# FFN of a two-layer hybrid decoder step: where the sums of the weight blocks stand in VectorE's and ScalarE's queues

## The chip, the cores and the metric

The kernel runs on one core of one Trainium2 chip (trn2). The metric is the time of one execution in device microseconds; of several runs the median is taken. A profiled execution is one further run, taken by the hardware profiler, and its time differs a little from the median.

## The reference

The program is one inference step of a small decoder: layer 0 mixes tokens with an mLSTM, layer 1 with latent attention, and behind each stands a SwiGLU FFN. There are 1024 prompt tokens and 8 new tokens of sampled sequences; in the kernel they stand side by side, 1032 columns. Only the FFN is touched by the change:

```python
def swiglu(x, w_gate_up, w_down):
    g, u = jnp.split(x @ w_gate_up, 2, axis=-1)
    return (jax.nn.silu(g) * u) @ w_down

hp = hp + swiglu(rmsnorm(hp, norm_ffn[layer]), ffn_w_gate_up[layer], ffn_w_down[layer])
hs = hs + swiglu(rmsnorm(hs, norm_ffn[layer]), ffn_w_gate_up[layer], ffn_w_down[layer])
```

Everything is float32. The model width is 1024, the FFN's inner width is 2816, that is 22 blocks of 128.

## The kernel before

**Arithmetic.** A float32 product is made of three matmuls in the format fp32r: both operands are split into a high part (ScalarE, `split`, L117: a copy that rounds) and a low part (VectorE, L118: source less high part), and `mm3` (L134 to L136) adds high x high, high x low and low x high. On top of that both projections of the FFN use a scheme of seven products for a 2 x 2 block product instead of eight (Strassen's, in Winograd's form): the seven left operands are four blocks of weights and sums of them, the seven right operands are blocks of activations and sums of them.

**Gate and up.** `gate_up(wg, f, parts, down)` makes block f of the 22 (called tile f here). Its two weight blocks, for gate and for up, are loaded by SyncE's queue into tiles `wr` (two buffers). From their quarters a11, a12, a21, a22 the function `operands` makes the seven operands: a11 and a12 as they are, then S = a21 + a22 (L1009) and S3 = a11 - a21 (L1010), S - a11 (L1014), a12 - S (L1017), and a22. Each is split into `wh`, `wl` or `w`. The order of the seven products is that of `PRODUCTS`: 0 and 4 (a11, a12), 3 (S - a11, here "the third product"), 1 (S), 2 (S3), 5 (a22), 6 (the last sum). Each product is made for two parts of the tokens, i = 0 (2 x 256 columns) and i = 1 (2 x 260), with 12 matmuls each, into PSUM banks `sc`. After each product the bank is read: by a copy on ScalarE (L1053, L1058, L1060) or by an instruction of VectorE (L1055, L1061, L1063, L1065, L1067); L1063 is the multiplication after product 5. The results are tiles `u`.

**Down.** The down projection takes the blocks of `u` in pairs (f, f + 1). `spread` makes the seven right operands `b` of a pair from its four `u` blocks by sums (L1075 to L1081) and splits. `down` is a generator: for each pair and each of four column blocks (a down tile) it makes 14 steps e, product e // 2 in the order of `PRODUCTS` for part e % 2, with 3 matmuls each, into banks `mm` and `ss`, and reads the banks (L1135 to L1146). The gate/up tile that runs at the time calls one step after every two of its groups of matmuls (28 steps a tile), so that the down projection of pair n runs in the middle of the gate/up tiles of later pairs; tile 3 calls them faster (54 steps). `down_raw` loads the weights of the next down tile into `dr` (one buffer) and makes their sums `dS` (L1096 to L1099) right behind it, at step 0; `down_put` splits A, B, D and C at steps 6, 9, 12 and 13. At the end of a down tile GpSimd issues a DMA that adds the result to the residual stream in memory (L1147).

**What sets the order.** Each engine works its queue strictly in order, and the order is made when the program is built: a scheduler takes the instructions by the order of the code and by its own estimate of when their operands are there. Where its estimate of a load is too short, an instruction stands in the queue ahead of others that could run. `tc.issue_after(ins)` orders every instruction made inside its block behind `ins` if it runs on the engine of `ins`; no wait on the chip comes with it.

**The start of the FFN.** `gate_up_half` makes tiles 0 and 1 for part 0 with plain products, and beside it VectorE and ScalarE make the right operands `c...` and `f...` of the other part from x (`forms`, L920 to L923; the last low half is `c5l`). Then `ffn` calls `spread` for the first pair's part 0, then tile 2 for both parts, then tiles 0 and 1 for part 1. Tiles `u` have four tags, and a tag is used again by a later block (`rows`).

Of the kernel before, what the change touches and what calls it, by code (L numbers as in the profile page):

```python
# [1 line left out]

# [1 line left out]

# [9 lines left out]
ALU = mybir.AluOpType  # L14
# [4 lines left out]
P = 128  # L19
D = 1024  # L20
KT = D // P
S = 1024
# [9 lines left out]
PW = (256, 260)  # L32
# [59 lines left out]
class Kern:  # L92
# [888 lines left out]


    def rows(self, f, i):
        x = self.t(self.gu, [P, 2, PW[1]], "u%d%d" % ((1, 0) if (f, i) == (0, 1) else (f % 2, i)))[:, :, :PW[i]]
        self.u[f, i] = x
        return x


    def operands(self, wg, f):
        nc = self.nc  # L990
        A = []
        for c0 in (f * P, DFF + f * P):
            raw = self.t(self.wp, [P, KT * P], "wr")
# [12 lines left out]

        G = nc.vector.tensor_tensor
        s, s3 = (self.t(self.gu, [P, 4, P], "S", bufs=2) for i in range(2))
        G(s, a21, a22, op=ALU.add)  # L1009
        G(s3, a11, a21, op=ALU.subtract)  # L1010
        yield put(a11)
        yield put(a12)
        s1 = put(s)
# [9 lines left out]
    def gate_up(self, wg, f, parts, down=iter(()), skip=0, steps=(1, 1)):  # L1023
# [8 lines left out]
        for s, bank, first in PRODUCTS:  # L1032
            ahead.append(next(ops, None))
            w = ahead.pop(0)
            for i in parts:
# [16 lines left out]
                if s == 0:  # L1052
                    nc.scalar.copy(u[:, 0], ps)  # L1053
                elif s == 4:
                    V.tensor_tensor(u[:, 0], u[:, 0], ps, op=ALU.add)  # L1055
                    nc.scalar.activation(u[:, 0], u[:, 0], AF.Silu)
                elif s == 3:
                    nc.scalar.copy(x, ps)  # L1058
                elif s == 2:
                    nc.scalar.copy(u[:, 1], ps)  # L1060
                    V.tensor_tensor(u[:, 1], u[:, 1], banks[i, 1], op=ALU.add)  # L1061
                elif s == 5:
                    V.tensor_tensor(u[:, 0], u[:, 0], ps, op=ALU.mult)  # L1063
# [23 lines left out]


    def down_raw(self, wd, f0, dp):
        nc = self.nc  # L1090
        G = nc.vector.tensor_tensor
        raw = self.t(self.fp, [P, 2, 2 * P], "dr")
        nc.sync.dma_start(raw, self.wsrc(wd, f0 * P, 2, dp * 2 * P, 2 * P))
        a11, a21, a12, a22 = (raw[:, k, r * P:r * P + P] for k in range(2) for r in range(2))
        S = self.t(self.fp, [P, 4, P], "dS")
        G(S[:, 1], a21, a22, op=ALU.add)  # L1096
# [3 lines left out]
        return {"A": raw[:, :, 0:P], "B": S[:, 0:2], "C": S[:, 2:4], "D": raw[:, 1:2, P:]}  # L1100


    def down_put(self, src, n):
# [6 lines left out]
    def down(self, wd):  # L1110
        nc = self.nc
        V = nc.vector
        todo = [(f0, dp) for f0 in range(0, NF - 4, 2) for dp in range(KT // 2)]
        src = self.down_raw(wd, *todo[0])
        W = {n: self.down_put(src, n) for n in "ABCD"}
        st0 = [self.t(self.wp, [P, KT * P], "wl", F32R).bitcast(F32) for _ in range(2)]
        yield
        for n, (f0, dp) in enumerate(todo):
# [7 lines left out]
            for e in range(14):  # L1126
# [11 lines left out]
                elif s == 3:  # L1138
                    nc.scalar.copy(c[:, 0, 1], ps)
                elif s == 2:  # L1140
                    nc.scalar.copy(c[:, 1, 1], ps)
                    V.tensor_tensor(c[:, 1, 1], c[:, 1, 1], banks[i][1], op=ALU.add)
                elif s == 5:
                    nc.scalar.copy(c[:, 1, 0], ps)
                elif s == 6:
# [873 lines left out]
```

## Time and profile before

| what | us |
|---|---|
| median of 3 runs | 2722.95 (2720.21 to 2729.66) |
| the profiled execution, whole | 2727.58 |
| its span, from the first to the last instruction | 2725.8 |
| TensorE (PE) busy | 2538.9 |
| VectorE (DVE) busy | 1859.1 |
| ScalarE (ACT) busy | 1327.4 |
| mean granted clock of TensorE | 0.973 of full |

In the profile's rows a line such as L1009 is a line of the kernel, `S<-wr` says which tile is written and which are read, buffer numbers left out. Times are counted from the start of the span. A matmul's busy time is modelled and overlaps the next one's start: in a full stretch a matmul with 256 columns is busy for 0.28 us and the next starts 0.12 us later. "[3.81 <-DMA wr]" is idle time of the engine ahead of this instruction, with what ended it. The first layer's FFN lies between about 536 and 1160 us, the second's between about 2012 and 2640 us.

### The profile page before, as it was taken

To read this page: it belongs to the slowest core of one execution; us is meant where nothing else is said; L and a number is where in the kernel's file an instruction comes from. 1 tells how busy PE (TensorE), PEld (TensorE's weight loads), DVE (VectorE), ACT (ScalarE), POOL (GpSimd) and SP (SyncE) were. 2 spreads that over 40 slices of the span, in tenths; PEclk is the share of its full clock that TensorE was granted. 3 is DMA by queue.
4 is the path that set the end of the run, shared out by engine and by line. 5 is a ranking of instruction groups with operands and counts; after the bars stand their busy time and mean duration, and the time that the engine had idled before them with its cause. 6 is when DMAs were issued, how large, how long until landed. Compare 5 with 4: busy or idle time off the path is not lost.

```text
span 2725.8 us, 54325 instructions
## 1 busy us (share of the span) xinstructions
PE 2538.9 (93%) x21151; PEld 2389.8 (88%) x21151; DVE 1859.1 (68%) x4490; ACT 1327.4 (49%) x3280; POOL 576.3 (21%) x582
## 2 busy tenths in 40 slices
PE   8999998989999999999887888888989999999998
PEld 8998887989999999999875667677789999999998
DVE  4345568887777777666556776768497777777755
ACT  4212234456555556453354455546255655655543
POOL 1000102201111111122334444442310111111102
PEclk9999989999999999999998999989999999999999
DMA  5133445526656656653666666653624755666553
GB/s 187 39 69 84 124 141 121 160 63 129 127 120 122 124 110 121 118 157 97 239 226 238 227 237 220 222 200 124 201 90 97 138 110 115 131 123 120 114 126 120
DMA packets 341992, 383.37 MB, mean 141 GB/s; under 512 B 23417, under 2 KB 274686, under 8 KB 333414
## 3 DMA queue, kind: packets, MB, share of 16 engines
q0 software_dynamic: 59520, 183.34, 28.8%
q1 hardware_dynamic: 257814, 180.21, 22.2%
q10 hardware_dynamic: 24400, 16.36, 2.4%
q8 instruction: 166, 2.72, 0.4%
q14 instruction: 92, 0.75, 0.1%
HBM read 254.12 MB, written 125.70 MB: 139 GB/s over the span
## 4 chain that ended last, share of the span: by engine, by line
PE 62%; DVE 16%; DMA 11%; ACT 5%; issue 3%; POOL 1%; another core or an unknown queue 0%; SPq 0%; ACTq 0%; POOLq 0%; DVEq 0%
PE sc L136 12%; PE sc L134 11%; PE sc L135 11%; PE mm L134 5%; PE mm L136 5%; PE mm L135 4%; DMA wr<-in_ffn_w_gate_up_dram 3%; DVE tt L1797 2%; PE ss L1829 2%; DMA Gb<-G_d 2%; PE ss L134 2%; PE ss L136 2%; PE ss L135 2%; DVE wl L118 2%; PE ss L1804 1%
## 5 line engine op out<-in xcount | busy, mean ns | idle before, releaser
L1147 POOL DMA_DIRECT2D x_d<-wl x72 | 86.7, 1205 | 1046.3 <-DVE wl L1146 367.4
L117 ACT ACTIVATE wh<-wr 128x512 fp32r<-128x512 f32 (+2 forms) x170 | 137.5, 810 | 225.5 <-PE mm L135 133.2
L1797 DVE STREAM_TRANSPOSE tt<-nat 128x1024 f32<-128x1024 f32 x128 | 153.9, 1223 | 9.5 <-PE ss L1804 6.1
L118 DVE TENSOR_TENSOR wl<-wr,wh 128x1024 fp32r<-128x1024 f32 (+2 forms) x83 | 99.8, 1203 | 39.5 <-ACT wh L117 31.2
L117 ACT ACTIVATE b<-u 128x256 fp32r<-128x256 f32 (+1 forms) x252 | 97.8, 414 | 43.6 <-DVE u L1063 29.7
L134 PE MATMUL mm<-zh,wh 128*128 128x344 f32 x320 | 105.3, 329 | 7.2 <-DVE ot L462 7.2
L1804 PE MATMUL ss<-tt,qbd 128*32 128x128 f32 x2560 | 92.7, 281 | 17.2 <-DVE tt L1797 12.2
L118 DVE TENSOR_TENSOR b<-u,b 128x256 fp32r<-128x256 f32 (+1 forms) x252 | 104.6, 422 | 1.4 <-ACT b L117 1.3
L135 PE MATMUL mm<-zl,wh 128*128 128x344 f32 x320 | 104.4, 326 | 0.0
L136 PE MATMUL mm<-zh,wl 128*128 128x344 f32 x320 | 104.2, 326 | 0.0
L1804 PEld LDWEIGHTS ss<-tt,qbd 128*32 128x32 f32 x2560 | 71.7, 112 | 34.0 <-DVE tt L1797 21.0
L1147 POOL DMA_DIRECT2D x_d<-st x72 | 99.1, 1376 | 4.4 <-DVE dC L118 3.5
L117 ACT ACTIVATE wh<-S 128x512 fp32r<-128x512 f32 x108 | 68.3, 633 | 47.7 <-PE sc L136 33.4
L118 DVE TENSOR_TENSOR wh<-S,wh 128x512 fp32r<-128x512 f32 x108 | 74.2, 689 | 22.1 <-ACT wh L117 21.0
L1700 PE MATMUL mm<-wh,vt 128*128 128x256 f32 (+1 forms) x320 | 75.6, 298 | 11.1 <-ACT wh L117 5.2
L134 PE MATMUL sc<-zh,wh 128*128 128x344 f32 x256 | 84.1, 329 | 1.3 <-ACT wh L117 1.1
L136 PE MATMUL sc<-zh,wl 128*128 128x344 f32 x256 | 83.3, 325 | 0.7 <-DVE wl L118 0.7
L135 PE MATMUL sc<-zl,wh 128*128 128x344 f32 x256 | 83.2, 325 | 0.0
L118 DVE TENSOR_TENSOR wh<-wr,wh 128x512 fp32r<-128x512 f32 x85 | 58.5, 688 | 26.5 <-ACT wh L117 26.4
L1659 ACT ACTIVATE wr<-sc,mx,rqt 128x512 f32<-128x512 f32 (+2 forms) x96 | 64.1, 673 | 22.5 <-DVE mx L1654 12.6
L1700 PEld LDWEIGHTS mm<-wh,vt 128*128 128x128 f32 x320 | 56.1, 197 | 21.6 <-ACT wh L117 8.7
L1789 POOL DMA_INDIRECT nat<-in_cache_latent_dram,idx x64 | 61.2, 957 | 61.8 <-PE ss L1829 48.2
(1052 smaller groups left out, 10703.2 us busy)
## 6 DMA issues: line engine op xcount, KB each, us to landing
wr<-in_ffn_w_gate_up_dram SPq DMA_DIRECT2D x96, 512.0 KB
x_d<-st POOLq DMA_DIRECT2D x72, 520.0 KB
x_d<-wl POOLq DMA_DIRECT2D x72, 512.0 KB
dr<-in_ffn_w_down_dram SPq DMA_DIRECT2D x72, 256.0 KB
wr<-in_mlstm_w_in_dram SPq DMA_DIRECT2D x24, 512.0 KB
wr<-in_mlstm_w_out_dram SPq DMA_DIRECT2D x16, 512.0 KB
wr<-in_mla_w_o_dram SPq DMA_DIRECT2D x15, 512.0 KB
q<-qn_d SPq DMA_DIRECT2D x28, 256.0 KB
```

The costliest lines, as they stand in the source:

```text
L117: ins = nc.scalar.activation(hi, src, AF.Copy)
L118: self.low = e.tensor_tensor(lo, src, hi.bitcast(F32), op=ALU.subtract)
L134: mm(ps, wh, xh, start=start, stop=False, **kw)
L135: mm(ps, wh, xl, start=False, stop=False, **kw)
L136: self.last = mm(ps, wl, xh, start=False, stop=stop, **kw)
L1147: nc.gpsimd.dma_start(self.x_d[:, 2 * dp:2 * dp + 2, 512 * i:512 * i + 2 * PW[i]], st[i], accum_op=ALU.add)
L1659: nc.scalar.activation(px[:, ks], o, AF.Exp, bias=mx[:, 0:1], scale=f, accum_out=sm[:, c:c + 1])
L1700: nc.tensor.matmul(o, x, y, start=i == 0, stop=i == len(ops) - 1)
L1789: nc.gpsimd.indirect_dma_start(out=nat[:, s].rearrange("p s c -> p (s c)"), out_offset=None, in_=lat, in_offset=ix)
L1797: V.transpose(out=tt, in_=src.rearrange("p s (c i) -> p c s i", i=32))
L1804: nc.tensor.matmul(psS[32 * j:32 * j + 32, u * P:u * P + P], self.qbd[:, b, cb], tt[:, c, 4 * j:4 * j + 4].rearrange("p s k -> p (s k)"), ...
L1829: nc.tensor.matmul(psV[32 * j:32 * j + 32], pz[:, j, i], keys[i // 4][:, j * 4 + i % 4], start=i == 0, stop=i == 7)
```

## The change

Four things are edited. In `operands` the first two sums S and S3 of every tile f > 3 are ordered behind `self.pin`, the multiplication after product 5 of part 0 of the tile before. In `down` the sums of the next down tile's weights are no longer made at step 0, with the load, but at step 8, ordered behind the two instructions (ScalarE's copy `y` and VectorE's addition `x`) that read the bank of that step; the split of A is made there too (it was at step 6), that of B at step 10 (it was at step 9). The first pair's combinations for part 0 are no longer called before tile 2: tile 2 gets them as its generator and calls one after every two groups of matmuls, from the seventh call on. And the tags of the tiles `u` are dealt out differently, so that tile 2 does not write to the buffers of the first pair.

```diff
     def rows(self, f, i):
-        x = self.t(self.gu, [P, 2, PW[1]], "u%d%d" % ((1, 0) if (f, i) == (0, 1) else (f % 2, i)))[:, :, :PW[i]]
+        x = self.t(self.gu, [P, 2, PW[1]], "u%d%d" % ((0, f) if f < 2 else (1 - f % 2, i)))[:, :, :PW[i]]
...
         s, s3 = (self.t(self.gu, [P, 4, P], "S", bufs=2) for i in range(2))
-        G(s, a21, a22, op=ALU.add)
-        G(s3, a11, a21, op=ALU.subtract)
+        with self.tc.issue_after(self.pin) if f > 3 else nullcontext():
+            G(s, a21, a22, op=ALU.add)
+            G(s3, a11, a21, op=ALU.subtract)
...
                 elif s == 5:
-                    V.tensor_tensor(u[:, 0], u[:, 0], ps, op=ALU.mult)
+                    ins = V.tensor_tensor(u[:, 0], u[:, 0], ps, op=ALU.mult)
+                    if i == parts[0]:
+                        self.pin = ins.ins
...
     def down_raw(self, wd, f0, dp):
         raw = self.t(self.fp, [P, 2, 2 * P], "dr")
+        self.nc.sync.dma_start(raw, self.wsrc(wd, f0 * P, 2, dp * 2 * P, 2 * P))
+        return {"A": raw[:, :, 0:P], "D": raw[:, 1:2, P:], "raw": raw}
+
+
+    def down_sums(self, src):
+        G = self.nc.vector.tensor_tensor
+        a11, a21, a12, a22 = (src["raw"][:, k, r * P:r * P + P] for k in range(2) for r in range(2))
         S = self.t(self.fp, [P, 4, P], "dS")
         G(S[:, 1], a21, a22, op=ALU.add)
         G(S[:, 0], S[:, 1], a11, op=ALU.subtract)
         G(S[:, 2], a11, a21, op=ALU.subtract)
         G(S[:, 3], a12, S[:, 0], op=ALU.subtract)
+        src.update(B=S[:, 0:2], C=S[:, 2:4])
...
                 elif s == 2:
-                    nc.scalar.copy(c[:, 1, 1], ps)
-                    V.tensor_tensor(c[:, 1, 1], c[:, 1, 1], banks[i][1], op=ALU.add)
+                    y = nc.scalar.copy(c[:, 1, 1], ps)
+                    x = V.tensor_tensor(c[:, 1, 1], c[:, 1, 1], banks[i][1], op=ALU.add)
...
                 if more and e == 0:
                     src = self.down_raw(wd, *todo[n + 1])
-                if more and e in (6, 9, 12, 13):
-                    x = {6: "A", 9: "B", 12: "D", 13: "C"}[e]
+                if more and e == 8:
+                    with self.tc.issue_after(x.ins), self.tc.issue_after(y.ins):
+                        self.down_sums(src)
+                        W["A"] = self.down_put(src, "A")
+                if more and e in (10, 12, 13):
+                    x = {10: "B", 12: "D", 13: "C"}[e]
                     W[x] = self.down_put(src, x)
...
-        for _, x, i in SPREAD:
-            if i == 0:
-                self.spread(0, x, i)
-        self.gate_up(wg, 2, (0, 1))
+        self.gate_up(wg, 2, (0, 1), (self.spread(0, x, i) for _, x, i in SPREAD if i == 0), 6)
```

GpSimd's and SyncE's instructions stand in the same order as before. On VectorE and ScalarE the FFN's instructions are reordered, on TensorE a few are.

VectorE's queue, before, around the sum S of gate/up tile 10 of the first layer (S_9224). Here u_8846 and u_8882 are tile 9's results for part 0 and part 1, wl_6158 and st_9049 the down projection's results, dA and dB its weights.

```order
L1061 TENSOR_TENSOR u_8882<-u_8882,sc_8915 128x260
L1009 TENSOR_TENSOR S_9224<-wr_9222 128x512
L118 TENSOR_TENSOR dA_9138<-dr_9056,dA_9138 128x256
L1010 TENSOR_TENSOR S_9225<-wr_9220,wr_9222 128x512
L1063 TENSOR_TENSOR u_8846<-u_8846,sc_8817 128x256
L118 TENSOR_TENSOR wh_9228<-wr_9220,wh_9228 128x512
L118 TENSOR_TENSOR b_9141<-u_8846,b_9141 128x256
L118 TENSOR_TENSOR b_9153<-u_8440,b_9153 128x256
L1063 TENSOR_TENSOR u_8882<-u_8882,sc_8849 128x260
L118 TENSOR_TENSOR wh_9231<-wr_9220,wh_9231 128x512
```

The same place of VectorE's queue in the changed kernel; line numbers from L1009 on are larger by one to seven there, u_8877 is what was u_8882, and L1064 is what was L1063.

```order
L1062 TENSOR_TENSOR u_8877<-u_8877,sc_8910 128x260
L118 TENSOR_TENSOR wh_9228<-wr_9220,wh_9228 128x512
L1064 TENSOR_TENSOR u_8846<-u_8846,sc_8817 128x256
L1010 TENSOR_TENSOR S_9224<-wr_9222 128x512
L1011 TENSOR_TENSOR S_9225<-wr_9220,wr_9222 128x512
L118 TENSOR_TENSOR b_9133<-u_8846,b_9133 128x256
L118 TENSOR_TENSOR b_9145<-u_8440,b_9145 128x256
L1064 TENSOR_TENSOR u_8877<-u_8877,sc_8849 128x260
L118 TENSOR_TENSOR wh_9231<-wr_9220,wh_9231 128x512
L118 TENSOR_TENSOR b_9168<-u_8477,b_9168 128x260
L118 TENSOR_TENSOR b_9182<-u_8877,b_9182 128x260
L1149 TENSOR_TENSOR wl_6158<-wl_6158,ss_9048 128x256
```

The low half of the first weights (wh_9228) and part 0's multiplication now stand ahead of the sum, the low half of dA (dA_9138 before) has gone behind it, and part 1's multiplication is still behind it.

TensorE's queue, before, at the first products of tile 2 of the first layer; sc_5649 and the other sc tiles are its banks, dA_6145 the down projection's first weights, b_5603 and b_5607 the first pair's right operands.

```order
L134 MATMUL sc_5681<-f4h_5074,w_5639 128x256
L135 MATMUL sc_5681<-f4l_5075,w_5639 128x256
L134 MATMUL sc_5696<-c4h_5574,w_5639 128x260
L135 MATMUL sc_5696<-c4l_5575,w_5639 128x260
L134 MATMUL mm_6225<-b_5603,dA_6145 128x256
L135 MATMUL mm_6225<-b_5603,dA_6145 128x256
L134 MATMUL ss_6226<-b_5607,dA_6145 128x256
L135 MATMUL ss_6226<-b_5607,dA_6145 128x256
L136 MATMUL sc_5649<-f0h_4927,wl_5636 128x256
L134 MATMUL sc_5649<-f0h_4927,wl_5636 128x256
```

The same place in the changed kernel (sc_5656 is what was sc_5681, sc_5671 what was sc_5696, wl_5611 what was wl_5636):

```order
L134 MATMUL sc_5656<-f4h_5074,w_5614 128x256
L135 MATMUL sc_5656<-f4l_5075,w_5614 128x256
L134 MATMUL sc_5671<-c4h_5574,w_5614 128x260
L135 MATMUL sc_5671<-c4l_5575,w_5614 128x260
L136 MATMUL sc_5624<-f0h_4927,wl_5611 128x256
L134 MATMUL sc_5624<-f0h_4927,wl_5611 128x256
```

The four matmuls with dA have gone to a later place, among the first products of tile 3; tile 2's own products follow each other.

VectorE's queue at the same time, before: c5l is the last low half of `forms`, wl_5636 the one that the matmul L136 above reads.

```order
L118 TENSOR_TENSOR c5l_5586<-x_4738,c5h_5585 128x1040
L1009 TENSOR_TENSOR S_5632<-wr_5630 128x512
L118 TENSOR_TENSOR b_5603<-u_5286,b_5603 128x256
L118 TENSOR_TENSOR b_5607<-u_5438,b_5607 128x256
L1075 TENSOR_TENSOR u_5286<-u_5286 128x256
L118 TENSOR_TENSOR b_5625<-u_5438,b_5625 128x256
L1079 TENSOR_TENSOR u_5286<-u_5438,u_5286 128x256
L118 TENSOR_TENSOR b_5610<-u_5286,b_5610 128x256
L1010 TENSOR_TENSOR S_5633<-wr_5628,wr_5630 128x512
L1077 TENSOR_TENSOR u_5286<-u_5438,u_5286 128x256
L118 TENSOR_TENSOR b_5619<-u_5286,b_5619 128x256
L1081 TENSOR_TENSOR u_5438<-u_5438,u_5286 128x256
```

And in the changed kernel:

```order
L118 TENSOR_TENSOR c5l_5586<-x_4738,c5h_5585 128x1040
L1010 TENSOR_TENSOR S_5607<-wr_5605 128x512
L1011 TENSOR_TENSOR S_5608<-wr_5603,wr_5605 128x512
L118 TENSOR_TENSOR wl_5611<-wr_5603,wl_5611 128x512
L118 TENSOR_TENSOR w_5614<-wr_5603,w_5614 128x512
L118 TENSOR_TENSOR wh_5617<-S_5607,wh_5617 128x512
L118 TENSOR_TENSOR b_5678<-u_5286,b_5678 128x256
```

Before, wl_5636 came next behind the last row shown, with nine instructions of the first pair and the two sums between c5l and it; now the two sums alone stand between, and the pair's instructions are behind.

More of the change, by code (lines that the diff above doesn't have):

```diff
@@ L1 @@
-from contextlib import ExitStack
+from contextlib import ExitStack, nullcontext
 import numpy as np
@@ L1089, in down_raw @@
     def down_raw(self, wd, f0, dp):
-        nc = self.nc
-        G = nc.vector.tensor_tensor
         raw = self.t(self.fp, [P, 2, 2 * P], "dr")
-        nc.sync.dma_start(raw, self.wsrc(wd, f0 * P, 2, dp * 2 * P, 2 * P))
-        a11, a21, a12, a22 = (raw[:, k, r * P:r * P + P] for k in range(2) for r in range(2))
+        self.nc.sync.dma_start(raw, self.wsrc(wd, f0 * P, 2, dp * 2 * P, 2 * P))
[3 more added lines that the diff above has]
+        a11, a21, a12, a22 = (src["raw"][:, k, r * P:r * P + P] for k in range(2) for r in range(2))
         S = self.t(self.fp, [P, 4, P], "dS")
@@ L1099, in down_raw @@
         G(S[:, 3], a12, S[:, 0], op=ALU.subtract)
-        return {"A": raw[:, :, 0:P], "B": S[:, 0:2], "C": S[:, 2:4], "D": raw[:, 1:2, P:]}
+        src.update(B=S[:, 0:2], C=S[:, 2:4])
     def down_put(self, src, n):
@@ L1149, in down @@
                     src = self.down_raw(wd, *todo[n + 1])
-                if more and e in (6, 9, 12, 13):
-                    x = {6: "A", 9: "B", 12: "D", 13: "C"}[e]
+                if more and e == 8:
+                    with self.tc.issue_after(x.ins), self.tc.issue_after(y.ins):
+                        self.down_sums(src)
+                        W["A"] = self.down_put(src, "A")
+                if more and e in (10, 12, 13):
+                    x = {10: "B", 12: "D", 13: "C"}[e]
                     W[x] = self.down_put(src, x)
```

## The prediction

> **What bounds the kernel now.** The page first: which engine the time belongs to.
>
> ```profile
> span 2725.8 us, 54325 instructions
> PE 2538.9 (93%) x21151; PEld 2389.8 (88%) x21151; DVE 1859.1 (68%) x4490; ACT 1327.4 (49%) x3280; POOL 576.3 (21%) x582
> ```
>
> TensorE is busy for 93% of the span, VectorE for 68%. So a VectorE instruction costs time only where TensorE stands still for it, and I look for those places in the two FFN stages, the only ones that the change touches. The table by stretches shows one stretch of 60 us that is full and the next, with the same work, that is not (columns: length, busy us and count of PE, PEld, DVE, ACT, POOL, granted clock, DMA share, GB/s):
>
> ```profile
> 700.00:760.00 60.00, 59.75 (x503) 59.55 (x502) 45.56 (x122) 36.01 (x96) 9.72 (x8) 1.00 0.59 115
> 760.00:820.00 60.00, 58.32 (x487) 57.70 (x486) 43.68 (x114) 33.73 (x91) 7.54 (x7) 1.00 0.60 120
> ```
>
> Next the waits of TensorE alone, in the first layer's FFN (536 to 1160 us) and in the second's (2012 to 2640 us); columns: total us, times, longest:
>
> ```profile
> PE mm L134 <- ACT dA L117: 7.1, 1, 7.1
> PE mm L134 <- ACT wl L1141: 5.0, 4, 2.1
> PE sc L134 <- ACT wh L117: 2.2, 4, 0.7
> PE sc L136 <- DVE wh L118: 1.3, 3, 0.4
> PE ss L134 <- DVE st L1137: 0.7, 1, 0.7
> ```
>
> ```profile
> PE mm L134 <- ACT dA L117: 7.4, 1, 7.4
> PE sc L134 <- ACT wh L117: 2.9, 5, 0.8
> PE mm L134 <- ACT wl L1141: 2.7, 4, 0.7
> PE sc L136 <- DVE wh L118: 1.8, 4, 0.4
> ```
>
> Three kinds: one long stop at the start of each FFN (dA), eight stops for an eviction of the down projection (L1141), and as many places where the third product of a gate/up tile waits for its weights (wh). The waits of VectorE name what lies behind the second and third kind:
>
> ```profile
> DVE S L1009 <- DMA wr<-in_ffn_w_gate_up_dram: 64.1, 31, 3.8
> ...
> DVE dS L1096 <- DMA dr<-in_ffn_w_down_dram: 28.0, 33, 2.0
> ```
>
> VectorE stands for 92 us in front of sums whose weights are still being loaded, and whatever is queued behind them stands too. The chain of waits gives such loads' issue and length, the longest among them:
>
> ```profile
> 758.14 6.43 DMA wr<-in_ffn_w_gate_up_dram
> 820.52 7.91 DMA wr<-in_ffn_w_gate_up_dram
> ```
>
> **One stop in full.** The timeline around gate/up tile 10, VectorE, then ScalarE, then TensorE:
>
> ```profile
> 824.23 0.42 DVE L1061 TENSOR_TENSOR u<-u,sc 128x260 f32<-128x260 f32 x1
> 828.45 0.69 DVE L1009 TENSOR_TENSOR S<-wr 128x512 f32<-128x512 f32 x1 [3.81 <-DMA wr<-in_ffn_w_gate_up_dram]
> ...
> 830.00 0.41 DVE L1063 TENSOR_TENSOR u<-u,sc 128x256 f32<-128x256 f32 x1
> 830.33 0.69 DVE L118 TENSOR_TENSOR wh<-wr,wh 128x512 fp32r<-128x512 f32 x1
> 830.93 0.76 DVE L118 TENSOR_TENSOR b<-u,b 128x256 fp32r<-128x256 f32 x2
> ...
> 843.94 0.69 DVE L118 TENSOR_TENSOR wh<-S,wh 128x512 fp32r<-128x512 f32 x1
> ```
>
> ```profile
> 830.45 0.72 ACT L117 ACTIVATE b<-u 128x256 fp32r<-128x256 f32 x2 [4.21 <-DVE u L1063]
> ...
> 832.52 0.35 ACT L1141 COPY wl<-mm 128x256 f32<-128x256 f32 x1
> ```
>
> ```profile
> 802.15 0.28 PE L134 MATMUL sc<-f0h,w 128*128 128x256 f32 x1
> ...
> 832.92 0.39 PE L134 MATMUL mm<-b,dD 128*128 128x256 f32 x1 [2.13 <-ACT wl L1141]
> ...
> 835.14 0.41 PE L134 MATMUL sc<-f0h,wh 128*128 128x256 f32 x1
> ...
> 865.92 0.28 PE L134 MATMUL sc<-f0h,wh 128*128 128x256 f32 x1
> ...
> 874.46 0.28 PE L134 MATMUL sc<-f3h,wh 128*128 128x256 f32 x1
> ...
> 889.49 0.28 PE L134 MATMUL sc<-c5h,wh 128*128 128x260 f32 x1
> ...
> 895.90 0.28 PE L134 MATMUL sc<-f0h,w 128*128 128x256 f32 x1
> ```
>
> The load is issued at 820.52 and lands at 828.43; the sum starts at 828.45, with the multiplication L1063 behind it, ScalarE's split b behind that, and the copy L1141 behind that; TensorE wants the bank of this copy. Each row with f0h is the start of a tile: tiles 9 and 10 take 32.99 and 30.78 us, the undisturbed tile 11 takes 29.98. The pair loses 3.8 us.
>
> **The change part by part.** *The gate/up sums, where their load is late (tiles 8, 10, 14, 16 of each layer, eight in all).* The sums are pinned behind part 0's multiplication (L1063), which so stands ahead of the wait, with the low half of the next tile's first weights. But the load lands when it did, since its issue hangs on a buffer that TensorE frees, and POOL's and SP's instructions keep their order. So the sum starts at the same 828.45 and VectorE still waits, from about 826. The first stop shrinks: behind the sum stand a second sum (0.60), two splits (0.34 each) and part 1's multiplication (0.41), so ScalarE's copy comes near 831.1 and TensorE 0.4 later (as at 832.52 and 832.92), 1.4 us sooner than before. That is not the gain, since the third product is late next: it needs the low half of S, which VectorE starts 15.49 us behind the sum (828.45 to 843.94). What the change takes out of this stretch is one low half (830.33 to 830.93, 0.60) and one multiplication (830.00 to 830.33, 0.33); the rest is only put in another order. With some 0.3 to 0.4 us of short waits that may go too, the stretch becomes 14.2 to 14.6 us, and each pair is shorter by 0.9 to 1.3 us; I take 1.1, the middle. 8 x 1.1 = 8.8 us.
>
> *The same sums in tiles 4, 6, 12 and 18 of each layer.* Here nothing is late now. Pinned, the sum can start when the sixth product's part 0 is done (889.49 in a clean tile), matmul, multiplication and latency later, 890.2; plus 14.2 and 0.7 until TensorE can use the half (low half to matmul as at 564.80 and 565.54, below) is 905.1. TensorE wants it, by the clean tile, 8.54 + 0.24 us behind its start, at 904.7. So these tiles keep or get a stop of about 0.4 us where they have one of about 0.4 now: nothing, bounds 2.4 us to either side (8 x 0.3).
>
> *The down sums* go from behind their load to behind the eviction of down step 8, with dA's split; SP's loads keep their place. A tile has 28 such steps in 29.98 us, so eight are 8.6 us, longer than the longest load above; the cover behind is six steps, 6.4 us, for about 2 us of copy, sums and split. If that cover were gone, each of the 70 boundaries between down tiles would pay. The 28.0 us of VectorE idle go; TensorE waits directly for that only in the st stop (0.7, with 0.16 for the pipelined matmul 0.9), in the down's quick stage. I count that 0.9.
>
> *The first pair's combinations.* The start of the FFN:
>
> ```profile
> 560.58 0.68 DVE L1009 TENSOR_TENSOR S<-wr 128x512 f32<-128x512 f32 x1
> ...
> 564.80 0.69 DVE L118 TENSOR_TENSOR wl<-wr,wl 128x512 fp32r<-128x512 f32 x1
> ```
>
> ```profile
> 563.75 0.58 PE L134 MATMUL mm<-b,dA 128*128 128x256 f32 x1 [7.13 <-ACT dA L117]
> ...
> 565.54 0.58 PE L136 MATMUL sc<-f0h,wl 128*128 128x256 f32 x1 [0.57 <-DVE wl L118]
> ```
>
> ```profile
> 564.00:570.65 6.65, 6.08 (x27) 5.78 (x28) 6.11 (x15) 2.73 (x7) 0.00 (x0) 0.50 0.00 0
> 833.50:837.00 3.50, 3.50 (x19) 3.50 (x18) 3.32 (x10) 2.28 (x7) 0.00 (x0) 0.52 0.00 0
> ```
>
> TensorE starts eight matmuls of tile 2, then four of the down projection that need dA, then waits for wl. Now the four are gone from here (they come later, 4 x 0.12 = 0.5 us), and wl is third behind the sums: 560.58 + 2 x 0.60 = 561.78 instead of 564.80, so TensorE goes on at 562.5 instead of 565.5. The stop shrinks from 7.1 us to about 6, not to nothing: VectorE's c5l still comes before. The clock stands at half after it (0.50 to 570.65, a matmul each 0.21 us instead of 0.12). If it stays at half for as long as now, 6.9 us from the restart, 42 matmuls are done by 570.65 instead of 24 and the four: 14 x 0.12 = 1.7 us. If it stays at half up to the same moment, 1.2. The second layer alike, so 1.7 x 2 = 3.4; bounds 2.4 and, with the clock full early, 5.4.
>
> The Trainium skill, "TensorE: Matmul & The Clock Gate", Part 1, has the clock fall after an idle window of about 3.4 us and rise after as much work. The second row above speaks against the first half: 0.52 after a stop of 2.13 us. By that rule the slow stretch at 833.5 is not the stop's doing and would stay when the stop shrinks (1.2 us there: 3.50 less 19 x 0.12); by the row it goes. The sum without that gain would be 1.2 smaller, 11.9, and 2711.1; I go by the row, and count nothing twice, as the 1.1 us of the pair hold it.
>
> Sum: 8.8 + 0.9 + 3.4 = 13.1 us. Nothing else moves: first and last tiles, attention and mixers keep their order. The profiled execution took 2727.58 us in all (1.8 beside its span) and would take 2714.5; it lies 4.6 above the median of the three runs, 2722.95. Against that median, I forecast 2709.9 us.
>
> **The rivals.** *No gain in the tiles (not slower).* The third product's weights stay as late as they are, because ScalarE's queue, not VectorE's work, holds the high half in front; then only the start of each FFN gains, 2.4 to 3.4 us: 2720. For it: the stop "sc L134 <- ACT wh", 5.1 us in both layers, is on the high half. Against it: that half waits for a sum that VectorE makes.
>
> *Slower.* The pin is too late: in all 16 even tiles VectorE needs x us more than 14.2 between sum and third product, because evictions that it now meets there are not ready. Each us costs 16 us, less 13 gained: from x = 0.8 on the change loses, and at x = 1.5, 24 - 13 = 11, 2734. For it: in tiles 4, 6, 12 and 18 the sum now starts later than before, and by the working above comes 0.4 us too late at best. Against it: VectorE has 14 us free of each 60.
>
> *The clock rises sooner.* At the FFN's start the half clock lasts 3.5 us from 562.5, as long as the stretch from 833.5, and not 6.9: 16 slow matmuls, then 39 quick ones by 570.65, 55 instead of 28, which is 3.2 us a layer and 6.4 instead of 3.4 in all: 2706.9. For it: the row of 3.50 us at 0.52; against it: the row of 6.65 us at 0.50, at this very place. The Trainium skill, "TensorE: Matmul & The Clock Gate", Part 1, would have it so: about 3.4 us of work bring the full clock back.
>
> **How the numbers follow.** A measurement of this kernel tells about 0.3% (8.2 us) from no change, so "faster" begins below 2714.8. The forecast has 0.57, the sooner clock 0.10, no gain in the tiles 0.25, slower 0.08. The forecast's own bounds: 0.9 x 8 or 1.3 x 8 in the first term, 2.4 either way in the second, 2.4 to 5.4 at the starts; together 8 to 20 us with two or three at an end: 2703 to 2715. The range takes in the clock's case, and of the case without gain all but its top: 2699 to 2721. Faster 0.65 (nearly all of the first two cases), same 0.28, slower 0.07.
>
> **What would show it.** Right: TensorE's wait for L1141's copy (then L1148) falls from 7.7 us in both layers to about 1; its waits for wh stay at several us; VectorE's wait for wr stays in eight tiles, at 1 to 2.5 us each, and that for dr is gone; the stop at the FFN's start is 6 us and names wl, not dA; tile pairs 9 and 10 take about 62.5 us instead of 63.8. Wrong: waits for wh gone (the stretch is far below 14 us, a larger gain), grown in tiles 6, 12, 18 (the pin is too late), a new wait for dA at a down tile's first step, or full clock at the FFN's start.

## The result, and the profile after

The changed kernel takes 2703.3 us (median of 6 runs, 2699.0 to 2709.4), the kernel before in the same series 2723.25 (6 runs, 2719.3 to 2729.7). The ratio is 0.9925, 95% interval 0.9907 to 0.9944: 20 us or 0.75% faster, between 15 and 25. The forecast was 13 us faster, the range 2 to 24.

The page of the changed kernel, its head and two of its engines' lines; TensorE does the same work in a shorter span:

```profile
span 2703.0 us, 54247 instructions
PE 2539.4 (94%) x21151; PEld 2393.8 (89%) x21151; DVE 1855.5 (69%) x4490; ACT 1326.0 (49%) x3280; POOL 574.8 (21%) x582
```

TensorE's waits in the first layer's FFN of the changed kernel (total us, times, longest), then in the second's, and VectorE's wait for the gate/up weights:

```profile
PE sc L136 <- DVE wl L118: 5.9, 1, 5.9
...
PE mm L134 <- ACT wl L1148: 2.5, 1, 2.5
PE sc L136 <- DVE wh L118: 1.0, 3, 0.3
...
PE sc L134 <- ACT wh L117: 0.4, 2, 0.2
```

```profile
PE sc L136 <- DVE wl L118: 5.9, 1, 5.9
...
PE sc L136 <- DVE wh L118: 1.3, 4, 0.3
...
PE sc L134 <- ACT wh L117: 0.4, 2, 0.2
```

```profile
DVE S L1010 <- DMA wr<-in_ffn_w_gate_up_dram: 32.0, 26, 4.3
```

The eight stops for the copy of wl (7.7 us) have become one of 2.5; the stops for wh have fallen from 8.2 us to 3.1; the stop at each FFN's start is 5.9 us and names wl. VectorE's wait for wr has halved (64.1 before), that for dr is not listed any more.

**How a tile looks now.** VectorE, then TensorE, around gate/up tile 8 of the first layer:

```profile
755.04 0.69 DVE L1010 TENSOR_TENSOR S<-wr 128x512 f32<-128x512 f32 x1 [0.97 <-DMA wr<-in_ffn_w_gate_up_dram]
...
769.25 0.69 DVE L118 TENSOR_TENSOR wh<-S,wh 128x512 fp32r<-128x512 f32 x1
```

```profile
760.21 0.28 PE L134 MATMUL sc<-f0h,wh 128*128 128x256 f32 x1
...
769.05 0.39 PE L134 MATMUL sc<-f3h,wh 128*128 128x256 f32 x1
...
769.99 0.39 PE L136 MATMUL sc<-f3h,wh 128*128 128x256 f32 x1 [0.32 <-DVE wh L118]
```

The stretch from the sum to the third product's low half is 14.21 us, at the edge of the forecast's 14.2 to 14.6. The half is still late: the L136 of the third product comes 9.78 us behind the tile's start, where a clean tile has it at 8.54 + 0.24 = 8.78.

**Where the time came from.** Two lengths can be read from any of these traces. One is that of the 16 gate/up tiles 4 to 19, from the first matmul with f0h of tile 4 to that of tile 20; in the first layer before, and then after:

```profile
648.90 0.28 PE L134 MATMUL sc<-f0h,wh 128*128 128x256 f32 x1
...
1143.04 0.28 PE L134 MATMUL sc<-f0h,wh 128*128 128x256 f32 x1
```

```profile
639.94 0.28 PE L134 MATMUL sc<-f0h,wh 128*128 128x256 f32 x1
...
1129.41 0.28 PE L134 MATMUL sc<-f0h,wh 128*128 128x256 f32 x1
```

That is 494.14 and 489.47 us; with the second layer (492.68 and 485.29) the 32 tiles take 986.8 before and 974.8 after. The other length is that of the start, from the first matmul with c4h ahead of the long stop to tile 4; its first end in the first layer, before and after:

```profile
556.11 0.39 PE L134 MATMUL sc<-c4h,w 128*128 128x260 f32 x1 [0.20 <-DVE u L980]
```

```profile
550.89 0.39 PE L134 MATMUL sc<-c4h,w 128*128 128x260 f32 x1 [0.20 <-DVE u L980]
```

Over both layers the starts take 183.4 us before (92.79 + 90.60) and 177.6 after (89.05 + 88.56). So the FFN gained 12.0 + 5.8 = 17.8 us. The spans differ by 22.8: the two rows show 5.2 us more that lie ahead of the first FFN, in code that the change does not touch (in the profiles of e1 to e4 this row stands at 544.31 to 548.80, so such a difference belongs to the execution). The two lengths were read in every profile:

```
kernel                        ratio to before [95%]     32 tiles   2 starts
before                        1                          986.8      183.4
changed                       0.9925 [0.9907, 0.9944]    974.8      177.6
e1   pin alone                0.9959 [0.9945, 0.9973]    979.3      183.4
e2   down sums alone          0.9974 [0.9962, 0.9986]    979.2      181.8
e3   first pair alone         0.9984 [0.9969, 0.9998]    987.6      179.9
e4   changed, pin later       0.9901 [0.9884, 0.9918]    964.2      178.7
e5   e4, TensorE's order back 0.9957 [0.9944, 0.9969]    981.9      176.9
e6   before, order late       0.9979 [0.9967, 0.9991]    979.5      183.5
e7   changed, order late      0.9911 [0.9893, 0.9930]    966.5      178.3
e8   changed, sub early       0.9915 [0.9895, 0.9935]    969.3      177.4
e9   changed, once more       0.9921 [0.9903, 0.9940]    974.9      177.0
e10  later pin alone          0.9931 [0.9909, 0.9952]    971.4      183.0
e11  e4, wl first             0.9886 [0.9863, 0.9909]    964.1      176.0
```

Three chips took part: beside e1 to e4 the kernel before took 2721.3 us, beside e5 to e8 2693.8, beside e9 to e11 2696.5. Ratios are therefore compared, not times. The FFN's lengths hardly depend on the chip: the changed kernel's 32 tiles took 974.8 on one and 974.9 on another.

### The profile page after: what moved, and what is told of

Read it like the earlier page. It is cut to its first block, busy times and chain, and to the rows that moved or that the text cites. A ratio compares the mean times of both kernels' runs of the same rounds, so it can differ in the third digit from the quotient of the medians.

```text
span 2703.0 us, 54247 instructions
## 1 busy us (share of the span) xinstructions
PE 2539.4 (94%) x21151; PEld 2393.8 (89%) x21151; DVE 1855.5 (69%) x4490; ACT 1326.0 (49%) x3280; POOL 574.8 (21%) x582
## 4 chain that ended last, share of the span: by engine, by line
PE 64%; DVE 17%; DMA 9%; ACT 4%; issue 3%; POOL 1%; SPq 0%; another core or an unknown queue 0%; ACTq 0%; POOLq 0%; DVEq 0%
PE sc L136 12%; PE sc L134 12%; PE sc L135 12%; PE mm L134 5%; PE mm L136 5%; PE mm L135 5%; DMA wr<-in_ffn_w_gate_up_dram 3%; DVE tt L1805 3%; PE ss L1837 2%; DMA Gb<-G_d 2%; PE ss L136 2%; PE ss L135 2%; PE ss L134 2%; PE ss L1812 1%; DVE wl L118 1%
## 5 line engine op out<-in xcount | busy, mean ns | idle before, releaser
L136 PE MATMUL mm<-zh,wl 128*128 128x344 f32 x320 | 104.3, 326 | 0.0
L136 PE MATMUL sc<-zh,wl 128*128 128x344 f32 x256 | 82.6, 323 | 0.5 <-DVE wl L118 0.5
L1149 DVE TENSOR_TENSOR wl<-wl,ss 128x256 f32<-128x256 f32 x72 | 30.2, 420 | 70.8 <-ACT wl L1148 70.7
L1667 ACT ACTIVATE wr<-sc,mx,rqt 128x512 f32<-128x512 f32 (+2 forms) x96 | 64.1, 672 | 22.3 <-DVE mx L1662 12.9
L1837 PE MATMUL ss<-nat,pz 128*32 128x256 f32 x1024 | 67.3, 400 | 7.0 <-ACT pz L1833 6.9
```

The source lines that it names most:

```text
L136: self.last = mm(ps, wl, xh, start=False, stop=stop, **kw)
L1149: x = V.tensor_tensor(c[:, 1, 1], c[:, 1, 1], banks[i][1], op=ALU.add)
L1667: nc.scalar.activation(px[:, ks], o, AF.Exp, bias=mx[:, 0:1], scale=f, accum_out=sm[:, c:c + 1])
L1837: nc.tensor.matmul(psV[32 * j:32 * j + 32], pz[:, j, i], keys[i // 4][:, j * 4 + i % 4], start=i == 0, stop=i == 7)
```

## Experiments

**One part of the change at a time.** The first theory was the prediction's: the pin pays in the tiles by taking VectorE work out of the stretch between the sum and the third product; the down sums pay almost nothing. Its rival turns this round. e1, the kernel before with the pin only:

```diff
-        G(s, a21, a22, op=ALU.add)
-        G(s3, a11, a21, op=ALU.subtract)
+        with self.tc.issue_after(self.pin) if f > 3 else nullcontext():
+            G(s, a21, a22, op=ALU.add)
+            G(s3, a11, a21, op=ALU.subtract)
```

> The kernel before with one edit of the change: S and S3 of the gate/up tiles f > 3 pinned behind the multiplication of part 0. Theory (what pays in the tiles is less VectorE work between the sum S and the third product, where the load is late): the stretch from S to the third product's low half falls from 15.5 to about 14 us in tiles 8, 10, 14 and 16 of both layers, and the kernel is 8 to 12 us faster than before (ratio 0.9956 to 0.9970); VectorE's waits for the down projection's weights stay at about 28 us. Rival (it is the 28 us of VectorE's idle time on those weights that pays, through the later place of the down sums): 0 to 3 us faster (0.999 to 1.000).

Measured: 11 us faster (0.9959, 7 to 15), 7.5 in the tiles. The stretch falls to 14.2 to 14.4 us in the eight tiles with a late load, as expected. VectorE's wait for the down weights does not stay at 28 us, it grows to 36.5; that for wr falls to 32.1, as in the changed kernel. TensorE's waits of e1 in the first layer, those for the copy and for wh, and then VectorE on the way to tile 6:

```profile
PE mm L134 <- ACT wl L1144: 3.0, 1, 3.0
PE sc L134 <- ACT wh L117: 2.0, 5, 0.7
PE sc L136 <- DVE wh L118: 1.8, 4, 0.4
```

```profile
689.99 0.29 DVE L1099 TENSOR_TENSOR dS<-dr 128x128 f32<-128x128 f32 x1 [0.87 <-DMA dr<-in_ffn_w_down_dram]
...
694.09 0.42 DVE L118 TENSOR_TENSOR dA<-dr,dA 128x256 fp32r<-128x256 f32 x1
694.43 0.41 DVE L1064 TENSOR_TENSOR u<-u,sc 128x256 f32<-128x256 f32 x1
694.76 0.68 DVE L1010 TENSOR_TENSOR S<-wr 128x512 f32<-128x512 f32 x1
```

Of the eight stops for the copy the pin alone leaves one (none is listed in the second layer); those for wh stay, 3.8 us in this layer against 3.5 before and 1.4 in the changed kernel. VectorE still waits 0.87 us for the down weights, and dA's low half stands ahead of the multiplication: from the wait to the sum there is work without a pause. The sum starts 5.66 us ahead of tile 6 (700.42), in the changed kernel 6.23 (693.86 and 700.09). Tile 6 takes 30.51 us here and 30.16 there.

e2, the kernel before with the down sums only:

```diff
-                if more and e in (6, 9, 12, 13):
+                if more and e == 8:
+                    with self.tc.issue_after(x.ins), self.tc.issue_after(y.ins):
+                        self.down_sums(src)
+                        W["A"] = self.down_put(src, "A")
+                if more and e in (10, 12, 13):
```

> The kernel before with one edit of the change: the sums of the down projection's weights at step 8 instead of step 0. Theory: VectorE's wait for the down weights goes (28 us to about 0), but TensorE hardly waits for it, so 0 to 2 us faster (0.9993 to 1.000), and TensorE's stops for the copy of wl stay at about 7.7 us over both layers. Rival (this move is what pays): 8 us or more faster (below 0.997).

Measured: 7 us faster (0.9974, 4 to 10); 7.6 in the tiles and 1.6 at the starts. The theory missed. The rival's "8 us or more" lies inside the interval, and the two lengths give 9.2: the move pays by itself, and about as much as the pin in the tiles. The stops for the copy, expected to stay at about 7.7 us over both layers, are 2.9. TensorE's waits of e2 in the first layer:

```profile
PE mm L134 <- ACT wl L1145: 2.7, 4, 1.4
PE sc L136 <- DVE wh L118: 1.3, 4, 0.3
...
PE sc L134 <- ACT wh L117: 0.8, 4, 0.2
```

The stops for the copy fell from 5.0 to 2.7 though nobody had pinned the gate/up sums, and those of ScalarE's wh from 2.2 to 0.8. 7.5 and 7.6 alone, 12.0 in the changed kernel: the two edits shorten the same stops in part.

e3, the kernel before with the first pair only:

```diff
-        for _, x, i in SPREAD:
-            if i == 0:
-                self.spread(0, x, i)
-        self.gate_up(wg, 2, (0, 1))
+        self.gate_up(wg, 2, (0, 1), (self.spread(0, x, i) for _, x, i in SPREAD if i == 0), 6)
```

> The kernel before with one edit of the change: the first pair's combinations made during tile 2. Theory: TensorE goes on 3.0 us earlier at the start of each FFN and its half clock there lasts 4 to 5 us; 2.3 to 3.2 us a layer, 5 to 6 us faster in all (0.9977 to 0.9982). Rival (as forecast, half clock for 6.9 us from the restart): 3.4 us faster. Second rival (the start's gain is given back at tile 3, where the down projection's first steps now stand): 0.

Measured: 4 us faster (0.9984, 0.5 to 8); the starts are 3.5 us shorter, the tiles 0.8 longer. The time alone does not tell 3.4 from 5.5; the starts' length stands with the 3.4 that the prediction forecast.

**How late may the sum be?** The prediction's slower rival priced a late pin at 16 us for each us. e4 is the changed kernel with the pin one multiplication later:

```diff
-                    if i == parts[0]:
+                    if i == parts[-1]:
                         self.pin = ins.ins
```

> The changed kernel with the pin one instruction later: S and S3 behind part 1's multiplication instead of part 0's, about 2.1 us later where the load is early, and 0.7 to 1.1 us less VectorE work between the sum and the third product. Theory (slack): in tiles 4, 6, 12 and 18, where the load is early, the third product's weights come 1 to 1.4 us later than TensorE wants them, so these eight lose 1 to 1.4 us each; in tiles 8, 10, 14 and 16 the shorter stretch gives 0 to 0.7 us. In all 3 to 10 us slower than the changed kernel, that is 10 to 17 us faster than before (0.9938 to 0.9963). Rival (the pin has room, and only the stretch behind a late load counts): faster than the changed kernel by 0 to 5 us, 20 to 25 us faster than before (0.991 to 0.9927).

Measured: 27 us faster than before (0.9901, 22 to 32), and its 32 tiles take 964.2 us, 10.6 less than the changed kernel's. The slack theory fell, and the rival's reason was not the right one either, as e5 shows. VectorE and TensorE around tile 8 in e4, then TensorE's waits in the first layer:

```profile
749.96 0.69 DVE L1010 TENSOR_TENSOR S<-wr 128x512 f32<-128x512 f32 x1
...
763.53 0.69 DVE L118 TENSOR_TENSOR wh<-S,wh 128x512 fp32r<-128x512 f32 x1
```

```profile
753.97 0.28 PE L134 MATMUL sc<-f0h,wh 128*128 128x256 f32 x1
...
763.09 0.28 PE L136 MATMUL mm<-b,dC 128*128 128x256 f32 x1
...
763.67 0.28 PE L134 MATMUL sc<-f3h,wh 128*128 128x256 f32 x1
```

```profile
PE sc L136 <- DVE wl L118: 5.9, 1, 5.9
PE sc L134 <- ACT u L1054: 3.1, 1, 3.1
PE sc L134 <- ACT w L117: 0.9, 1, 0.9
```

The low half starts 9.56 us behind the tile's start, later than in the changed kernel (9.04), and yet no stop at a third product is left (wl is the start of the FFN, w tile 3, u tile 20): the third product itself stands later, 9.70 us behind the start, with steps of the down projection (dB, dC) ahead of it. The scheduler, told by the later pin that the sum comes late, filled the time on TensorE.

The new theory: what a tile loses is the time at which the third product's weights are ready, less the time at which its turn comes in TensorE's queue; the pin moves both. Its rival: VectorE's queue is free of waits for loads in e4 (3.2 us in all against 32.0), and that is what pays. e5 keeps e4's pin and puts TensorE's order back:

```diff
-                            next(down, None)
+                            with self.tc.issue_after(last.ins) if s == 3 and f > 3 else nullcontext():
+                                next(down, None)
```

Here `last` is the last matmul of the group before, so that down steps called within the third product come behind it.

> The kernel with the later pin again, but the down steps called inside the third product are ordered behind the group of matmuls before them, so that TensorE's queue has the third product again right behind its first down step, as before the change; VectorE's and ScalarE's queues stay as with the later pin. Theory (the later pin gains because the scheduler, knowing of the later sum, put 9 to 12 matmuls of the down projection ahead of the third product): the low half still ends 10.0 to 10.3 us after the tile's start, TensorE wants it at about 9.0, and each of 16 even tiles loses 1.0 to 1.4 us again: 16 to 22 us slower than the later pin, 2 to 10 us faster than before (0.996 to 0.999). Rival (VectorE's queue, free of waits for the loads, is what pays): as the later pin, 24 to 27 us faster than before (0.990 to 0.991).

Measured: 0.9957 against e4's 0.9901, the 32 tiles 981.9 against 964.2: 17.7 us given back, 1.1 for each of 16 even tiles (by the time, 12 us faster than before, a little past the theory's 2 to 10). VectorE, TensorE around tile 8 and TensorE's waits in e5; VectorE's wait for its loads is as short as in e4:

```profile
DVE S L1010 <- DMA wr<-in_ffn_w_gate_up_dram: 3.9, 4, 1.2
```

```profile
756.92 0.28 PE L134 MATMUL sc<-f0h,wh 128*128 128x256 f32 x1
...
765.33 0.28 PE L136 MATMUL mm<-b,dB 128*128 128x260 f32 x1
766.50 0.39 PE L134 MATMUL sc<-f3h,wh 128*128 128x256 f32 x1 [0.88 <-ACT wh L117]
```

```profile
PE sc L134 <- ACT wh L117: 4.1, 5, 1.0
PE sc L134 <- ACT w L117: 3.6, 4, 0.9
```

The turn comes 8.5 us behind the start again, the weights at 9.6 as in e4 (VectorE starts the low half at 9.56 in both), and every even tile has its stop (31.1 to 31.5 us, 30.2 in e4). So the rival is out: with VectorE's waits gone, TensorE's order alone makes the difference.

The same from the other side: e6 is the kernel before, e7 the changed one, each with three down steps called ahead of the third product of even tiles, so that 9 matmuls (1.1 us) go ahead of it.

```diff
             w = ahead.pop(0)
+            for _ in range(3 if s == 3 and f > 3 and f % 2 == 0 else 0):
+                next(down, None)
+                done += 1
             for i in parts:
```

> The kernel before without any of the change, but in even tiles from 4 on three down steps (9 matmuls, 1.1 us) stand ahead of the third product in TensorE's queue. Theory (TensorE's order alone gives what the third product's stops cost): TensorE wants the low half at 9.85 us after the tile's start instead of 8.77, and it is there at 9.1 to 10.4; about 0.3 us in six tiles and 1.0 in ten: 10 to 12 us faster (0.9956 to 0.9963); the stops for the copy of wl stay at about 7.7 us. Rival (VectorE's work is what counts): 0 to 2 us.

Measured: 6 us faster (0.9979, 2 to 9), the tiles 7.3 shorter, less than expected. The even tiles gain 8.5 us (495.5 to 487.0), the odd ones, with the copies' stops, give back 1.2. The waits of e6 in the first layer show what the expectation left out:

```profile
PE mm L134 <- ACT wl L1144: 4.7, 4, 2.0
...
PE ss L134 <- DVE wl L1140: 1.0, 3, 0.5
...
PE sc L134 <- ACT wh L117: 0.3, 1, 0.3
```

Stops for wh went from 2.2 to 0.3, but the down steps put ahead now want banks that VectorE has not yet emptied (L1140). And the copies' stops stay: for these, VectorE's order is needed.

> The changed kernel with the same three down steps ahead of the third product. Theory: its seven stops of 0.8 to 1.5 us at the third product go, 6 to 7 us faster than the changed kernel, 26 to 27 us faster than before (0.990 to 0.9905). Rival (the time is given back further on, because the load stays late): as the changed kernel, 20 us faster than before (0.9925).

Measured: 0.9911. Its interval holds both expectations, so the time decides nothing; the tiles do: 966.5 us, 8.3 less than the changed kernel's, as the theory had it.

e8 moves the other term: the subtraction and its split are written ahead of the split of a12 becoming due.

```diff
-        yield put(a12)
+        w = put(a12)
         s1 = put(s)
         G(s, s, a11, op=ALU.subtract)
+        yield w
```

> The changed kernel with the subtraction S - a11 and the split of S written ahead of the split of a12, so that VectorE has 1.1 us less work between the sum and the third product's low half; TensorE's queue has the third product where it stood before. Theory (what the changed kernel still loses is the stretch on VectorE against TensorE's place for the third product): the stretch falls from 14.2 to 13.1 us, seven stops shrink by 0.8 to 1.0 each, 5 to 7 us faster than the changed kernel, 25 to 27 us faster than before (0.990 to 0.991). Rival (ScalarE's high half holds it): 0 to 2 us against the changed kernel, 0.992 to 0.9927 against before.

Measured: 0.9915, again not told apart by the time. The tiles take 969.3 us, 5.5 less than the changed kernel's; the stretch is 13.2 us in the tiles with a late load.

**The changed kernel again, the later pin alone, and a better start.** e9 repeats the changed kernel beside the next two.

> The changed kernel once more, on the same chip as the next two, so that they can be set against it: 19 to 21 us faster than before (0.992 to 0.9935), the 32 gate/up tiles 4 to 19 of both layers in 974 to 976 us.

Measured: 0.9921, tiles 974.9. e10 is e1 with the later pin, and nothing else of the change:

> The kernel before with one edit: S and S3 pinned behind part 1's multiplication; down sums and first pair as before. In TensorE's queue the third product of even tiles stands 3 to 5 matmuls later than before, not 9 to 12. Theory (what counts is how long before TensorE's turn the low half is ready): TensorE wants it 0.4 to 0.6 us later than before, it ends at about 10.0 to 10.3 us, each even tile loses 0.3 to 0.8 us against the later pin in the changed kernel; the 32 tiles take 969 to 977 us, 10 to 18 us faster than before (0.9935 to 0.9963). Rival (the down sums' place is needed, since VectorE would wait 30 us and more for their load): the 32 tiles take 980 us or more.

Measured: 19 us faster (0.9931, 13 to 25), tiles 971.4, 7.2 more than with the rest of the change (e4). Even tiles take 30.3 to 30.7 us but two, 32.95 and 31.31. The down sums are not needed for most of the gain; the tiles came out as expected, the time a little past the fast edge.

e11 is e4 with the splits of a11 and a12 of tile 2 ahead of the two sums:

```diff
+        if f == 2:
+            w = [put(a11), put(a12)]
         with self.tc.issue_after(self.pin) if f > 3 else nullcontext():
             G(s, a21, a22, op=ALU.add)
             G(s3, a11, a21, op=ALU.subtract)
```

> The kernel with the later pin, and in tile 2 the splits of a11 and a12 stand ahead of the two sums on VectorE, so that wl is first behind c5l and not third. Theory (the stop at the FFN's start ends with wl, 0.60 us for each instruction ahead of it): the stop falls from 5.9 to 4.7 us in both layers, 2.4 us faster than the later pin without it (0.989 to 0.9895 against before). Rival (the half clock after the stop takes the gain back, or c5l's own product comes late): 0.

Measured: 0.9886 (0.9863 to 0.9909), 31 us faster than before and 10.6 faster than the changed kernel beside it. VectorE's instruction next behind c5l and TensorE's restart at the first layer's start in e11, and the same place of the changed kernel:

```profile
549.12 0.68 DVE L118 TENSOR_TENSOR wl<-wr,wl 128x512 fp32r<-128x512 f32 x1
```

```profile
549.85 0.58 PE L136 MATMUL sc<-f0h,wl 128*128 128x256 f32 x1 [4.70 <-DVE wl L118]
```

```profile
555.35 0.69 DVE L1010 TENSOR_TENSOR S<-wr 128x512 f32<-128x512 f32 x1
...
556.55 0.69 DVE L118 TENSOR_TENSOR wl<-wr,wl 128x512 fp32r<-128x512 f32 x1
```

```profile
557.30 0.58 PE L136 MATMUL sc<-f0h,wl 128*128 128x256 f32 x1 [5.90 <-DVE wl L118]
```

The stop is shorter by the two sums, 2 x 0.60 = 1.2 us in each layer, and the starts are 2.7 us shorter than e4's. By its ratio e11 is the fastest kernel here, and it beats both kernels of the change. It is not told apart from e4 (0.9901): their intervals overlap, and they were not measured on one chip.

## Why the prediction was right, and which term was mis-sized

**Sign and mechanism held.** The load lands when it did (for tile 8, 24.8 us behind the start of tile 7 in both kernels), VectorE still waits for it, the first stop goes, and the third product is late next; 14.21 us of stretch were forecast as 14.2 to 14.6. Of the signs it named, the stop at the FFN's start (5.9 us, on wl), the stops for wh (3.1 us) and the end of the wait for dr came. The stops for the copy fell to 2.5 us, not to about 1, and one of the eight waits for wr was 4.3 us, not 1 to 2.5; both belong to tile 10 of the first layer. The size held only by the wide range: the forecast of 13 us lies below the measured 15 to 25.

**The gate/up sums (8.8 us, and nothing in tiles 4, 6, 12, 18).** e1 gives the pin alone 7.5 us over all 32 tiles, inside the bounds: the eight pairs with a late load gained 8.2, the other eight even tiles lost 0.7. In the changed kernel the stretch came out item by item as forecast: one low half, one multiplication and 0.2 to 0.4 us of short waits are gone from it. But the waits go with the down sums (e2's stretch has none and takes 15.13 us), so that part belongs to the next term; the pin alone leaves the waits, and reaches 14.2 because it also moves dA's low half (0.34 us) out of the stretch. In the changed kernel the eight pairs gained unevenly: tiles 9 and 10 of the second layer go from 62.44 to 60.96 us, those of the first from 63.77 to 64.12, since tile 10's load took 9.68 us there:

```profile
809.56 9.68 DMA wr<-in_ffn_w_gate_up_dram
```

```profile
822.33 0.58 PE L134 MATMUL mm<-b,dD 128*128 128x256 f32 x1 [2.50 <-ACT wl L1148]
```

Behind this load ScalarE's copy comes 2 to 3 us late, pin or not (2.13 us before, 3.01 in e1, 2.50 here); the forecast of 62.5 us for this pair failed by this stop, and by the slow stretch behind it, which the prediction had go and which stayed (the clock at 0.50 from 821.84 to 825.26).

**The down sums (0.9 us): this is the term that was mis-sized.** Alone they give 7.6 us in the tiles and 1.6 at the starts; beside the rest of the change what e1 and e3 leave is theirs: 12.0 - 7.5 = 4.5 in the tiles and 5.8 - 3.5 = 2.3 at the starts, 6.8 in all. The failing step is "TensorE waits directly for that only in the st stop": only the stop that names the result was priced. But VectorE's time in front of dr, and dA's low half, stood in the queue ahead of the multiplication and the gate/up sum, and what came late was put down to those. In e2 the eight pairs gained 5.2 us, and tiles 4, 6, 12 and 18 of both layers, which the prediction had at nothing, 2.4 (2.1 in the changed kernel): the third product's low half starts up to 1.5 us sooner there (tile 4 of the second layer, 10.10 us behind the tile's start before and 8.63 in e2).

**The first pair (3.4 us).** e3's starts are 3.5 us shorter, but that this is the forecast's size is in part luck: 2.5 us came in the first layer and 1.0 in the second, where the forecast had 1.7 in each. It took the second layer to be like the first, and before the change the half clock lasted 7.1 us from the restart in the first and 4.0 in the second; in e3 it lasted 6.0 and 5.1. In the changed kernel it lasted 5.1 and 4.2, between the forecast's 6.9 and the 3.5 of the rival "The clock rises sooner". The prediction's upper bound of 5.4 is not worked out, and that rival's 6.4 lies above it. The three parts, 7.5 + 6.8 + 3.5, make the 17.8 us of the FFN, since the middle one is what the others leave; the forecast had 8.8 + 0.9 + 3.4 = 13.1.

**The slower rival** named the right place and the wrong rule. "Each us costs 16 us" holds only with TensorE's queue as it is: e5, with that queue, loses 17.7 us against e4. But a pin also tells the scheduler that the sum is late, and then it moves the third product, too: the later pin was faster, not slower. The prediction worked out when the weights come and took the moment at which they are wanted as given.

**The rival "no gain in the tiles"** is out by 12 us of shorter tiles. What is open is why tile 10's load in the first layer is long (10.20 us in e1, 9.46 in e3, too); no run here tried it.

## What to carry to other kernels

A wait is worth the time at which an operand is ready less the time at which its turn comes in the consumer's queue: look at both ends, since an order constraint on the producer can make a scheduler refill the consumer's queue, and a later producer may then be the faster choice. Price the work that leaves a strict queue by all that stood behind it there, not only by the stop that names its result. Parts of a change that shorten the same stops do not add up: 7.5 and 7.6 alone were 12.0 in the changed kernel.

## What the runs showed of the hardware

The half clock behind the long stop lasts differently each time. From the restart to the first matmuls at 0.12 us it took between 3.2 and 7.5 us in the 26 starts of 13 profiles, and 4.0 and 3.2 us in the two layers of one execution (e5) after stops of the same 5.90 us. The longest (e6) and the shortest (e5), each at 0.50:

```profile
557.52:565.05 7.53, 6.96 (x31) 6.67 (x31) 6.36 (x16) 3.54 (x9) 0.00 (x0) 0.50 0.00 0
```

```profile
1993.28:1996.40 3.12, 3.12 (x14) 3.12 (x15) 3.12 (x7) 1.78 (x6) 0.00 (x0) 0.50 0.08 26
```

So neither 6.9 us nor 3.5 us is a property of this place, and one profile cannot price a shorter stop to better than 1 or 2 us. The traces' records of the granted clock show why. In all 13 executions every stretch at half clock within the two FFNs lasts 3.41, 6.83 or 10.24 us, whole multiples of 3.41, and within an execution all of them begin and end on one grid of that step, wherever the stops lie. What a stop costs thus depends on where on the grid it falls. A stop of 2.50 us was enough, and the clock fell about 2.0 us after it began, as these two stretches of the changed kernel around the stop that ended at 822.33 show (the clock is the third figure from the end):

```profile
818.43:821.84 3.41, 1.40 (x12) 1.19 (x10) 2.58 (x6) 0.24 (x1) 0.00 (x0) 1.00 0.13 25
821.84:825.26 3.42, 2.93 (x13) 2.93 (x14) 3.42 (x13) 1.94 (x7) 0.00 (x0) 0.50 0.00 0
```

In e1 a longer stop at the same place, 3.01 us, left the clock at 1.00 (815 to 835).

The Trainium skill, "TensorE: Matmul & The Clock Gate", Part 1, has about 3.4 us of idling ahead of the fall and about 3.4 us of work ahead of the rise. The traces show this length as the step of the grid (3.41 us), but not as a time counted from the stop: the fall came 2.0 us into a stop of 2.50, and the rise 3.2 to 7.5 us behind the restart.

The load of tile 10's weights in the first layer took 7.91 us before and 9.68 in the changed kernel; the other loads for tiles 8 to 16 that the two chains list took 6.4 to 7.3.
